# A two-block model in one kernel: handing out the second block's convolution by what is left, and moving eight copies to ScalarE

## The chip, the cores and the metric

The kernel runs on one core of one Trainium2 chip. The metric is device time in microseconds (us) of one execution, and lower is better. Before the change the median of three timed runs is 2483.45 us (2479.06 to 2487.06).

## The reference

The input is x, 512 positions by 1024 channels, float32. Two layers of a first block are followed by one layer of a second block.

A layer of the first block: RMS norm, one projection `h @ w_in`, and three branches, each gated and summed. They are a sliding-window attention with 8 heads, a short convolution of 3 taps, and a state-space model (SSM) with 32 groups of 64 complex states. Then comes a gated feed-forward of 2816 hidden channels.

The second block, cut to what matters here:

```python
h = rms_norm(x, pre_norm1) * (1 + sc1) + sh1
u_glu, q, k, v, gate_logits = split(h @ w_in_2)
u = ua * sigmoid(ub)                       # 1024 channels
u = depthwise_conv(u, 31 taps) + conv_b    # causal, along the 512 positions
u = silu(layer_norm(u, conv_ln_g, conv_ln_b))
y_conv = u @ conv_w_out_2 + conv_b_out
att = (softmax(q1 k1) - lam * softmax(q2 k2)) @ v    # causal, 8 heads
y_att = rms_norm(att, head_norm) * (1 - lam_init)
y = (sigmoid(g_conv) * y_conv + sigmoid(g_att) * y_att) @ w_o
x = x + g1 * rms_norm(y, post_norm1)
```

A feed-forward of 4096 hidden channels ends the block.

## The kernel before, in words

Activations lie with channels on the 128 partitions and positions along the row: eight tiles of 128 x 512, held in a pool of 78 equal slots of SBUF. Freed slots go to the end of a list, and new tiles take from its head. A float32 operand is split into a rounded high part and the rest (`split`, one ScalarE and one VectorE instruction), and a product is three matmuls (`mm3`, L470 to L472): high by high, high by low, low by high.

Weights come as a stream of units of 128 x 1024, three ahead, through rings of three buffers. SyncE loads a unit into `raw`, ScalarE writes the high part `wh`, and VectorE subtracts to get `wl`. For most of the second block's units `wl` is instead made by ScalarE and by a DMA from GpSimd's queue that adds the weights into it.

Beside the big products runs smaller work, written as Python generators that sit in lanes (class `Lane`): "bg" (first block's attention and SSM), "tab" (the SSM's tables, on GpSimd), "conv" and "att" (second block). `fm` and the other product loops call `beat()` after each group of matmuls, and every third beat is a tick. At a tick each lane gains its rate in credit and takes one step of its generators per whole credit. So the rates set where in program order the small work stands between the products. An order for each engine is then worked out by the framework's list scheduler, which takes instructions by program order but may issue a later one that it reckons ready earlier. SyncE keeps program order.

The second block's order: the gated linear units (GLU), whose last ten units run with the convolution lane already under way at rate 0.6 (R3); four parts, each with q, k and v for two heads; 16 gate units, all after part 3; `conv_w_out_2` (eight units), which needs the whole normalized convolution; `w_o_2`.

Counted in ticks by the loops: a part has 48 beats, so 16 ticks; the gates 128 beats, so 43 ticks; `conv_w_out_2` 64 beats, so 21 ticks.

- A channel tile's convolution (`convolve`) is one ScalarE instruction and 30 VectorE multiply-adds over 512 positions, with a step after every three: 10 steps a tile, 80 in all. A sum over the tiles, `csum`, is kept for the mean.
- `conv_norm` follows in the same lane: mean, eight steps of centring and squaring, one of the reciprocal root, and eight steps that scale, apply SiLU and split one tile each: 17 steps. What is left of the lane when the gates are done is issued at once by `finish("conv")`, ahead of `conv_w_out_2`.
- `diff_attention` of a part is one turn of q and k and four blocks of queries. With the steps that a waiting generator spends the four parts have 121 steps. The lane is two wide. Each part's attention is queued at the end of that part.

The rates before: "conv" 0.6 in the four parts (R4), 0.8 in the gates (R5); "att" 1.0 (R2), and 1.5 in `conv_w_out_2` (R6), where tile 6 calls `finish("att")` if attention isn't done.

In the first block `ssm` lays the input of a channel tile `ct` (0 to 3) out anew: 16 copies of 32 x 128, half on ScalarE, half on VectorE (L1176). GpSimd makes the tables of the next tiles meanwhile.

Of the kernel before, what the change touches and what calls it, by code (L numbers as in the profile page):

```python
# [13 lines left out]
AX = mybir.AxisListType  # L14


R1, R2, R3, R4, R5, R6 = 0.9, 1.0, 0.6, 0.6, 0.8, 1.5
T = 512
D = 1024
KD = 8  # L20
# [291 lines left out]
class Net:  # L312
# [839 lines left out]
    def ssm(self, L, ct, u, tabs, ys2):  # L1152
# [8 lines left out]
        bc, bl, cl, er, ei, rt = tabs[ct]  # L1161
# [9 lines left out]
        for i in range(4):  # L1171
            for j in range(4):
                o = uu[32 * j:32 * j + 32, i]
                s = u[32 * i:32 * i + 32, j::4]
                if j % 2:
                    nc.vector.tensor_copy(out=o, in_=s)  # L1176
                else:
                    self.act(o, s)
            if i == 1:
                yield  # L1180
# [191 lines left out]
    def second(self, follow, out):  # L1372
# [3 lines left out]
        conv = []  # L1376
        us = [None] * 8

        def convolve(i):
            acc = self.big(f"acc{i}")  # L1380
            self.act(acc, us[i], AF.Identity, scale=self.cw[:, 31 * i + 30:31 * i + 31], bias=self.p("conv_b", i))
            for j in range(29, -1, -1):
                s = 30 - j
                self.stt(acc[:, s:], us[i][:, :512 - s], self.cw[:, 31 * i + j:31 * i + j + 1], acc[:, s:], ALU.mult, ALU.add)
                if j % 3 == 0:
                    yield
            self.free(us[i])
            conv.append(acc)
            if i == 1:
                csum.append(self.big("csum"))  # L1390
                self.add(csum[0], conv[0], conv[1])
            elif i > 1:
                self.add(csum[0], csum[0], acc)

        csum, cn = [], []
        cl = self.lane("conv", 1, R3)
        ths = {}

# [12 lines left out]
        for i in range(GLU_HELD // 2):  # L1411
            cl.waiting.append(convolve(i))
        for i in range(GLU_HELD // 2, 8):
            w = self.unit("w_in_2")
            pb = self.psum("ub")
            self.fm(pb, w, 0, hs)
            t = self.big("th")
            self.act(t, pb, AF.Tanh, scale=0.5)
            w = self.unit("w_in_2")
            pa = self.psum("ua")  # L1420
            self.fm(pa, w, 0, hs)
            us[i] = self.big(f"uu{i}")
            self.stt(us[i], t, 1.0, pa, ALU.add, ALU.mult)
            self.free(pa, pb, t)
            cl.waiting.append(convolve(i))
            if i == GLU_HELD // 2:
                r1b = self.spread(self.r1)
                for k in range(8):
                    self.spill(k)
# [14 lines left out]
        def gate(m):  # L1444
            w = self.unit("w_in_2")
            pg = self.psum("gate")
            self.fm(pg, w, 0, hs)
            t = self.big("th")
            self.act(t, pg, AF.Tanh, scale=0.5)
            self.free(pg)  # L1450
            if m < 8:
                ga[m] = t
            else:
                gc.append(t)
            combine()
        al = self.lane("att", 2, R2)
        self.lane("conv", 1, R4)
        for part in range(4):
            pq = [self.psum(f"pq{t}") for t in range(NTB)]
            for i in range(4):  # L1460
                wh, wl, _ = self.unit("w_in_2")
                for t in range(NTB):
                    s = slice(128 * t, 128 * t + 128)
                    for e in range(2):
                        k = 2 * i + e
                        self.mm3(pq[t], hs[k][0][:, s], hs[k][1][:, s], wh[e], wl[e], k == 0, k == 7)
                        self.beat()
            ra = [self.big("rope", shape=(128, 8, 64)) for _ in range(NTB)]
            for t in range(NTB):
                self.act(ra[t].rearrange("p h d -> p (h d)"), pq[t])  # L1470
            self.free(pq)
            for t in range(NTB):
                self.rope2(ra[t], cos[:, t], sin[:, t])
            wv = [self.unit("w_in_2") for _ in range(2)]
            vv = []
            for t in range(NTB):
                if t % 2 == 0:
                    ps = self.psum("pv", (128, 2, 256))
                s = slice(128 * t, 128 * t + 128)
                for k in range(8):  # L1480
                    self.mm3(ps[:, t % 2], hs[k][0][:, s], hs[k][1][:, s], wv[k // 4][0][k % 4], wv[k // 4][1][k % 4],
                             k == 0, k == 7)
                    if k % 2:
                        self.beat()
                if t % 2:
                    vv.append(self.big("vv", shape=(128, 2, 256)))
                    self.act(vv[-1].rearrange("p t c -> p (t c)"), ps.rearrange("p t c -> p (t c)"))
                    self.free(ps)
            self.free(wv[0][2], wv[1][2])
            for m in (2 * part, 2 * part + 1):  # L1490
                ya[m] = self.big(f"ya{m}")
            al.waiting += self.diff_attention(part, ra, vv, ya, done)
            if part == 3:
                cl.waiting.append(self.conv_norm(conv, csum, cn))
                self.lane("conv", 1, R5)
            for m in range(sum(GATES[:part]), sum(GATES[:part + 1])):
                gate(m)
        self.free(hs, self.cs2)
        self.finish("conv")
        self.lane("att", 2, R6)  # L1500
        ys = []
        for m in range(8):
            w = self.unit("conv_w_out_2")
# [267 lines left out]
    def conv_norm(self, conv, csum, out):  # L1771
        while len(conv) < 8:
            yield
        s = csum[0]
        ps = self.psum("ssum", (128, 4))
        self.sums(ps, s)
        mu = self.small("mu", (128, 4))
        self.ts(mu, ps, 1.0 / D, ALU.mult)
        self.free(ps)
        mb = self.spread(mu)  # L1780
        st = [None]
        for i in range(8):
            self.sub(conv[i], conv[i], mb)
            self.sq_acc(st, conv[i])
            yield
        self.free(mb)
        rb = self.spread(self.rstd(st))
        yield
        for i in range(8):
            v = conv[i]  # L1790
            self.stt(v, v, self.p("ln_g", i), rb, ALU.mult, ALU.mult)
            t = self.big("th")
            self.act(t, v, AF.Tanh, scale=0.5, bias=self.hb[:, i:i + 1])
            self.act(v, v, AF.Identity, bias=self.p("ln_b", i))
            self.stt(v, t, 1.0, v, ALU.add, ALU.mult)
            h, l = self.big(f"cnh{i}", F32R), self.big(f"cnl{i}", F32R)
            self.split(h, l, v, 0.5)
            self.free(v, t)
            out.append((h, l))
            yield  # L1800
        self.free(rb)
# [49 lines left out]
```

## Time and profile before

| What | us |
|---|---|
| median of three timed runs | 2483.45 |
| lowest and highest | 2479.06, 2487.06 |
| the profiled execution, whole | 2489.97 |
| its span, first to last instruction | 2488.2 |
| TensorE busy (PE in the profile) | 2442.6 |
| VectorE busy (DVE) | 1594.7 |
| ScalarE busy (ACT) | 1111.5 |

The profile is one execution. PE is TensorE, PEld its loading of the stationary operand, DVE is VectorE, ACT is ScalarE, POOL is GpSimd, SP is SyncE. Times of rows count from the span's start. A figure in square brackets is idle time of the engine before a row, with what ended it. PEclk is the share of full clock that TensorE was granted. Where a helper issues an instruction, its line is the helper's: L380 is any ScalarE activation, L383 any two-tensor VectorE or GpSimd operation, L401 any scalar-tensor-tensor operation.

In the second block the GLU's last ten units run from 1643 to 1699 us, the four parts from 1699 to 1859, the gates from 1859 to 1978, and `conv_w_out_2` from 1996 to about 2069.

### The profile page before, as it was taken

To read this page: it belongs to the slowest core of one execution; us is meant where nothing else is said; L and a number is where in the kernel's file an instruction comes from. 1 tells how busy PE (TensorE), PEld (TensorE's weight loads), DVE (VectorE), ACT (ScalarE), POOL (GpSimd) and SP (SyncE) were. 2 spreads that over 40 slices of the span, in tenths; PEclk is the share of its full clock that TensorE was granted. 3 is DMA by queue.
4 is the path that set the end of the run, shared out by engine and by line. 5 is a ranking of instruction groups with operands and counts; after the bars stand their busy time and mean duration, and the time that the engine had idled before them with its cause. 6 is when DMAs were issued, how large, how long until landed. Compare 5 with 4: busy or idle time off the path is not lost.

```text
span 2488.2 us, 32578 instructions
## 1 busy us (share of the span) xinstructions
PE 2442.6 (98%) x12206; PEld 2054.3 (83%) x12206; DVE 1594.7 (64%) x3010; ACT 1111.5 (45%) x2034; POOL 362.5 (15%) x870
## 2 busy tenths in 40 slices
PE   8999999999999999999999999999999999999998
PEld 6888888888888888888888788988887769988887
DVE  7898855544455489875677744688788466643435
ACT  5467433322233365743432222544656765634222
POOL 7824000000037063200000000001111110000000
PEclk9999999999999999999999999999999989999999
DMA  4222233223233322123366632367646543122232
GB/s 154 80 77 69 77 123 106 93 94 102 93 99 109 120 70 79 60 102 121 130 208 223 216 120 94 116 168 182 147 102 140 119 106 119 69 93 89 93 106 77
DMA packets 90879, 282.80 MB, mean 114 GB/s; under 512 B 10336, under 2 KB 11744, under 8 KB 90720
## 3 DMA queue, kind: packets, MB, share of 16 engines
q1 hardware_dynamic: 83520, 254.50, 30.5%
q0 software_dynamic: 7200, 26.22, 6.2%
q8 instruction: 95, 1.56, 0.2%
q14 instruction: 64, 0.52, 0.1%
HBM read 274.39 MB, written 6.29 MB: 113 GB/s over the span
## 4 chain that ended last, share of the span: by engine, by line
PE 80%; DVE 7%; DMA 6%; issue 3%; ACT 2%; POOL 2%; SPq 1%; DVEq 0%; POOLq 0%; ACTq 0%
PE bank L470 25%; PE bank L471 25%; PE bank L472 25%; DMA slot<-in_wada_dram 4%; DVE slot L383 2%; DVE wl L383 2%; ACT slot L380 2%; PE bank L1712 1%; DVE slot L401 1%; DMA raw<-in_w_dram 1%; POOL s_w L383 1%; POOL slot L383 1%; PE bank L1744 1%; DVE slot L1176 0%; PE bank L1202 0%
## 5 line engine op out<-in xcount | busy, mean ns | idle before, releaser
L470 PE MATMUL bank<-slot,wh 128*128 128x512 f32 x2456 | 964.3, 394 | 7.8 <-ACT slot L380 7.6
L472 PE MATMUL bank<-slot,wl 128*128 128x512 f32 x2456 | 959.8, 391 | 4.2 <-DMA wl<-in_w_dram 2.1
L471 PE MATMUL bank<-slot,wh 128*128 128x512 f32 x2456 | 960.2, 391 | 0.0
L380 ACT ACTIVATE wh<-raw 128x1024 fp32r<-128x1024 f32 (+3 forms) x369 | 385.2, 1045 | 767.4 <-PE bank L471 390.6
L470 PEld LDWEIGHTS bank<-slot,wh 128*128 128x128 f32 x2456 | 463.4, 189 | 105.1 <-ACT slot L380 8.3
L472 PEld LDWEIGHTS bank<-slot,wl 128*128 128x128 f32 x2456 | 462.6, 188 | 104.5 <-DVE wl L383 4.9
L471 PEld LDWEIGHTS bank<-slot,wh 128*128 128x128 f32 x2456 | 463.4, 189 | 95.9 <-issue 1.7
L383 DVE TENSOR_TENSOR wl<-raw,wh 128x1024 fp32r<-128x1024 f32 (+3 forms) x319 | 390.9, 1226 | 203.0 <-ACT wh L380 201.6
L383 DVE TENSOR_TENSOR slot<-bank,slot 128x512 f32<-128x512 f32 (+4 forms) x340 | 197.6, 591 | 239.9 <-PE bank L472 208.7
L380 ACT ACTIVATE slot<-slot 128x512 fp32r<-128x512 f32 (+3 forms) x378 | 207.9, 558 | 288.9 <-DVE slot L383 265.9
L383 DVE TENSOR_TENSOR slot<-slot,slot 128x512 f32<-128x512 f32 (+4 forms) x480 | 287.0, 617 | 51.0 <-ACT slot L380 47.5
L380 ACT ACTIVATE slot<-bank 32x128 f32<-32x128 f32 (+8 forms) x398 | 183.2, 473 | 96.9 <-PE bank L472 34.5
L471 PE MATMUL bank<-wl,slot 128*128 128x512 f32 (+1 forms) x480 | 182.4, 380 | 4.3 <-DVE wl L383 4.3
L472 PE MATMUL bank<-wh,slot 128*128 128x512 f32 (+1 forms) x480 | 181.5, 379 | 0.0
L470 PE MATMUL bank<-wh,slot 128*128 128x512 f32 (+1 forms) x480 | 181.4, 380 | 0.0
L470 PE MATMUL bank<-slot,slot 128*128 128x256 f32 (+1 forms) x624 | 177.9, 293 | 2.1 <-ACT slot L380 2.1
L471 PE MATMUL bank<-slot,slot 128*128 128x256 f32 (+1 forms) x624 | 179.0, 291 | 0.5 <-DVE slot L401 0.5
L472 PE MATMUL bank<-slot,slot 128*128 128x256 f32 (+1 forms) x624 | 178.3, 289 | 0.0
L401 DVE SCALAR_TENSOR_TENSOR slot<-slot,slot 128x512 f32<-128x512 f32 (+1 forms) x184 | 123.9, 688 | 84.7 <-DMA slot<-in_wada_dram 57.2
L401 DVE SCALAR_TENSOR_TENSOR slot<-slot,cw,slot 128x485 f32<-128x485 f32 (+24 forms) x240 | 166.6, 732 | 4.2 <-ACT slot L380 2.4
L383 DVE TENSOR_TENSOR slot<-slot,bank 128x512 f32<-128x512 f32 (+1 forms) x104 | 66.1, 643 | 131.0 <-PE bank L472 131.0
L470 PEld LDWEIGHTS bank<-slot,slot 128*128 128x128 f32 x624 | 118.2, 193 | 4.4 <-ACT slot L380 2.7
(199 smaller groups left out, 2263.7 us busy)
## 6 DMA issues: line engine op xcount, KB each, us to landing
raw<-in_w_dram SPq DMA_DIRECT2D x373, 512.0 KB, 3.3
wl<-in_w_dram POOLq DMA_DIRECT2D x50, 512.0 KB, 5.6
slot<-in_wada_dram SPq DMA_DIRECT2D x96, 256.0 KB, 4.9
raw<-in_w_dram SPq DMA_DIRECT2D x32, 448.0 KB, 3.3
slot<-in_x_dram SPq DMA_DIRECT2D x16, 256.0 KB, 3.9
xd<-slot SPq DMA_DIRECT2D x16, 256.0 KB, 6.2
slot<-xd SPq DMA_DIRECT2D x16, 256.0 KB, 3.5
out_dram<-slot SPq DMA_DIRECT2D x8, 256.0 KB, 2.0
```

Of the source, the lines that this page charges most:

```text
L380: return self.nc.scalar.activation(out=out, in_=in_, func=func, scale=scale, **kw)
L383: return (eng or self.nc.vector).tensor_tensor(out=out, in0=a, in1=b, op=op)
L401: return self.nc.vector.scalar_tensor_tensor(out=out, in0=a, scalar=s, in1=b, op0=op0, op1=op1, **kw)
L470: t.matmul(ps, ah, bh, start=start, stop=False)
L471: t.matmul(ps, ah, bl, start=False, stop=False)
L472: t.matmul(ps, al, bh, start=False, stop=stop)
L1712: nc.tensor.matmul(ps[e][:, :w], qk[s][x][rows, tn], qk[2 + s][y][rows, :w], start=i == 0, stop=i == 2)
L1744: nc.tensor.matmul(po[:, e], at[e][:, b], vv[b // 2][:, b % 2, 128 * e:128 * e + 128], start=b == 0, stop=b == n)
```

## The change

Three things change. The convolution lane's rate is worked out ahead of each part as the steps still to do (`steps[0]`, 80 at first) over 16 ticks for each part left and 14 more; over 14 ahead of the gates; and `conv_norm` sets it to 0.7 when it starts. The attention lane keeps one rate, 1.25, to its end. In `ssm` the eight copies of tile `ct` 0 that VectorE made go to ScalarE, in both layers.

```diff
-R1, R2, R3, R4, R5, R6 = 0.9, 1.0, 0.6, 0.6, 0.8, 1.5
+R1, R2, R3 = 0.9, 1.25, 0.6
@@ ssm
-                if j % 2:
+                if j % 2 and ct:
                     nc.vector.tensor_copy(out=o, in_=s)
                 else:
                     self.act(o, s)
@@ convolve
                 if j % 3 == 0:
+                    steps[0] -= 1
                     yield
@@ second
+        steps = [80]
         cl = self.lane("conv", 1, R3)
...
         al = self.lane("att", 2, R2)
-        self.lane("conv", 1, R4)
         for part in range(4):
+            cl.rate = steps[0] / (16 * (4 - part) + 14)
...
             if part == 3:
                 cl.waiting.append(self.conv_norm(conv, csum, cn))
-                self.lane("conv", 1, R5)
+                cl.rate = steps[0] / 14
...
         self.finish("conv")
-        self.lane("att", 2, R6)
@@ conv_norm
         while len(conv) < 8:
             yield
+        self.lanes["conv"].rate = 0.7
```

## Rows read from the trace of the kernel before

**Rows 1.** The page's first part: busy time, share of span, instructions.
```profile
span 2488.2 us, 32578 instructions
PE 2442.6 (98%) x12206; PEld 2054.3 (83%) x12206; DVE 1594.7 (64%) x3010; ACT 1111.5 (45%) x2034; POOL 362.5 (15%) x870
```

**Rows 2.** Windows by stage; busy us and instructions of each engine, clock, DMA.
```profile
core 0: us, PE busy (x) PEld busy (x) DVE busy (x) ACT busy (x) POOL busy (x), PEclk, DMA share, GB/s
42.40:52.70 10.30, 6.04 (x28) 4.76 (x26) 10.17 (x10) 5.75 (x9) 10.30 (x28) 0.91 0.00 1
52.70:57.60 4.90, 4.90 (x12) 3.84 (x13) 3.56 (x2) 0.92 (x2) 4.90 (x9) 0.50 0.73 217
1643.40:1698.70 55.30, 55.30 (x244) 45.42 (x243) 53.18 (x83) 23.85 (x28) 7.73 (x9) 1.00 0.75 174
1698.70:1732.00 33.30, 33.30 (x193) 29.51 (x192) 31.91 (x55) 16.79 (x22) 4.32 (x5) 1.00 0.83 201
1732.00:1859.10 127.10, 127.10 (x760) 106.48 (x759) 96.79 (x224) 72.23 (x158) 15.64 (x17) 1.00 0.52 125
1859.10:1921.00 61.90, 61.90 (x303) 48.32 (x302) 54.76 (x106) 36.76 (x80) 9.04 (x10) 1.00 0.56 121
1921.00:1978.00 57.00, 56.98 (x277) 44.72 (x276) 24.95 (x78) 38.12 (x86) 8.46 (x10) 1.00 0.60 127
1978.00:1995.60 17.60, 8.58 (x59) 6.71 (x57) 12.74 (x32) 15.00 (x32) 3.61 (x4) 0.83 0.33 80
1995.60:1999.80 4.20, 4.16 (x9) 2.98 (x10) 2.71 (x6) 4.20 (x12) 0.00 (x0) 0.50 0.00 0
2023.70:2027.10 3.40, 3.40 (x10) 2.62 (x9) 0.34 (x1) 0.29 (x1) 0.86 (x1) 0.50 1.01 290
2064.60:2068.00 3.40, 3.40 (x18) 3.40 (x17) 3.40 (x6) 3.26 (x8) 0.00 (x0) 0.50 0.20 49
```

**Rows 3.** Timeline of DVE: start, time, form; the norm's last phase.
```profile
1985.89 4.73 DVE L401 SCALAR_TENSOR_TENSOR slot<-slot,slot,slot 128x512 f32<-128x512 f32 x7 [0.38 <-ACT slot L380]
```

**Rows 4.** Timeline of PE, 1952 to 2070 us; in brackets idle before.
```profile
1952.13 0.95 PE L597 MATMUL bank<-ones,slot 128*128 128x1 f32 x8
...
1992.08 0.69 PE L1712 MATMUL bank<-slot,slot 64*128 64x128 f32 x4 [4.50 <-DVE slot L383]
1995.62 0.80 PE L470 MATMUL bank<-slot,wh 128*128 128x512 f32 x1 [1.88 <-ACT slot L380]
...
2022.13 0.50 PE L472 MATMUL bank<-slot,wl 128*128 128x512 f32 x1 [2.12 <-DMA wl<-in_w_dram]
...
2064.07 1.18 PE L1744 MATMUL bank<-slot,slot 128*128 128x128 f32 x6 [2.61 <-ACT slot L380]
```

**Rows 5.** Timelines of DVE, ACT and PE around 45 us, layer 0.
```profile
42.37 8.29 DVE L1176 COPY slot<-slot 32x128 f32<-32x128 f32 x8
50.69 5.57 DVE L383 TENSOR_TENSOR wl<-raw,wh 128x1024 fp32r<-128x1024 f32 x3
...
44.51 1.06 ACT L380 ACTIVATE wh<-raw 128x1024 fp32r<-128x1024 f32 x1 [0.41 <-PE bank L472]
...
47.26 1.18 PE L470 MATMUL bank<-wh,slot 128*128 128x512 f32 x5
52.70 0.79 PE L471 MATMUL bank<-wl,slot 128*128 128x512 f32 x1 [4.26 <-DVE wl L383]
```

**Rows 6.** Tile cw, the convolution: ns min/median/max, first and last start.
```profile
L401 DVE SCALAR_TENSOR_TENSOR slot<-slot,cw,slot x240: 689/732/752, 1634.2 to 1919.2; 128x503 f32<-128x503 f32 x7, 128x497 f32<-128x497 f32 x7, 128x495 f32<-128x495 f32 x7, 128x493 f32<-128x493 f32 x7
```

**Rows 7.** Lines of DVE, 1564 to 2070 us: count, busy us, mean ns.
```profile
L552 DVE CUSTOM_DVE_ANT_0 slot<-bank,slot 128x128 f32<-128x128 f32 (+3 forms) x64 | 30.2, 487 | 32.5 <-PE bank L1712 32.3
L401 DVE SCALAR_TENSOR_TENSOR slot<-slot,dka,slot 128x128 f32<-128x128 f32 (+3 forms) x32 | 16.1, 546 | 0.0
```

**Rows 8.** The same copies elsewhere: eight on DVE, eight on ACT.
```profile
829.13 2.22 DVE L1176 COPY slot<-slot 32x128 f32<-32x128 f32 x8
...
926.22 3.52 ACT L380 ACTIVATE slot<-slot 32x128 f32<-32x128 f32 x8
```

## The prediction

> **What bounds the kernel now.** I read the page first: TensorE is busy 2442.6 of 2488.2 us [rows 1]. Making another engine cheaper gains nothing by itself; only TensorE's idle time, 45.6 us, and the stretches at half clock can be won. So I looked next at where TensorE idles in the stages that the change touches: the windows by stage, then its timeline there.
>
> From 1643 to 1978 us TensorE is idle for 0.02 us in all, though VectorE is busy 53.2 of 55.3 us in the last ten GLU units and 31.9 of 33.3 in part 0 [rows 2]. Then 17.6 us come in which TensorE has 8.6 us of work, so 9.0 idle [rows 2]. In that stretch VectorE and ScalarE work through the last phase of the convolution's norm [rows 3], which `finish("conv")` issues in one go after the gates; the first matmul of `conv_w_out_2` waits for ScalarE until 1995.62 [rows 4]. Two more waits follow: 2.12 us for a weight DMA, 2.61 us for attention's transposes at tile 6 [rows 4]. After each the granted clock is 0.50 for a while: 4.2, 3.4 and 3.4 us [rows 2]. At the lower of the two levels (1.2 against 2.4 GHz) half of each is lost: 2.1 + 1.7 + 1.7 = 5.5 us.
>
> In layer 0 TensorE waits 4.26 us at 52.70 for a weight's low part [rows 5], and 4.9 us at half clock follow [rows 2].
>
> **The change part by part.**
>
> *The convolution's rate.* Followed through the loops, 16 of the 80 steps are done when part 0 begins. Before, 0.6 x 64 ticks bring it to 54 at the gates' start; 26 steps and the 17 of the norm remain, and 43 ticks at 0.8 do 34 or 35, so 8 to 9 are left: the norm's whole last phase. After, the rate is 64 / 78 = 0.82 in all four parts and stays there, since each part works it out anew from what is left; the convolution is done 14 ticks into the gates, and the norm's 17 steps at 0.7 take 24 ticks. It ends at tick 38 of 43, and nothing is left to finish. Nothing is added to any engine. TensorE's gain is the 9.02 us of idle time and the 2.1 us of clock after it: 11.1. Bounds: 0, if the norm is still late, to 11.1.
>
> *What it costs in the parts.* 14.5 convolution steps move from the gates into the parts: 14.5 x 3 x 0.732 us [rows 6] = 31.8 us of VectorE. Attention adds 0.25 x 48 = 12 steps in parts 1 to 3. Its two dearest VectorE groups make (30.2 + 16.1) / 121 = 0.38 us a step [rows 7]; with the smaller operations I estimate 0.6, so 7 us. In the parts VectorE is busy 31.9 + 96.8 of 160.4 us, so 31.7 are idle [rows 2]. TensorE also gets 12 attention steps more there: parts 1 to 3 took 127.1 us against 3 x 33.3 for a part without attention, 27.2 us for 48 steps [rows 2], so 12 x 0.57 = 6.8 us. Demand 38.8, room 38.5: VectorE would be full. What it doesn't manage slips into the gates, where it has 61.9 + 57.0 - 54.8 - 25.0 = 39.1 us free before the norm's new work. That TensorE stays fed beside a VectorE at 96% is shown by the GLU units and part 0 [rows 2], but there nothing on TensorE waits for VectorE within a step; attention's scores do. No row shows a full VectorE beside attention. From below: no wait. From above: each of the 32 score pairs (64 maskings of L552 [rows 7]) waits for one convolution step of 3 x 0.732 = 2.2 us, 70 us. I take 4 us, near the lower end, as the stages closest in load have none; both ends go into the range.
>
> *Attention at 1.25.* Before, 91 ticks at 1.0 do 91 of 121 steps by the gates' end, and 30 are left for `conv_w_out_2`; at 1.5 a tick they aren't through at tile 6. After, 1.25 x 91 = 113 are done, and 8 are left, 7 ticks: under three tiles. The wait at 2064 and its clock go: 2.61 + 1.7 = 4.3 us. What is late next there is `w_o_2`'s first product, which needs tile 7, as it does now without a wait.
>
> *The weight wait at 2022.* ScalarE makes that unit's two halves in the same queue in which it is finishing the norm, and the DMA comes after them. With the norm done earlier ScalarE is free in time, as in the gates, where the same chain never stops TensorE [rows 2]. 2.12 + 1.7 = 3.8 us, between 0 and 3.8. These three places make 11.1 + 4.3 + 3.8 = 19.2 us; less 4, I take 15.
>
> *Eight copies to ScalarE.* In layer 0 VectorE's eight take 8.29 us; undisturbed eight take 2.22 [rows 8], and GpSimd is busy without a gap beside them [rows 2]. The `wl` subtractions stand behind them from 50.69, and TensorE ran out of work at 48.44 [rows 5]. Without the copies the first could start when ScalarE's `wh` is ready, at 45.57. But ScalarE now has the copies: eight take 3.52 us [rows 8]. It was idle 0.41 us ahead of `wh` [rows 5], so if all stand ahead, `wh` ends at 45.57 + 3.52 - 0.41 = 48.7, and `wl` 1.86 later (a third of 5.57 [rows 5]), at 50.5. TensorE, whose five high matmuls of 1.18 us also need that `wh`, then stops about 2.1 us in place of 4.26. If the scheduler puts `wh` between the copies it doesn't stop at all. So 2.2 to 4.3 us of idle time, and up to 2.4 of half clock [rows 2]; I take 5, between 2.2 and 6.7. In layer 1 the copies take 2.2 us on VectorE [rows 8] with no TensorE wait at that place: 0.
>
> The Trainium skill speaks against this part: "SBUF — State Buffer", section "Who interferes with whom", says that GpSimd shares one port pair with VectorE, that whoever comes first keeps it for a whole instruction, and that a VectorE instruction with two SBUF inputs contends too. By that the `wl` subtractions, which have two, would be held in the copies' place; it is the third rival. The trace agrees in part: three of them beside GpSimd took 5.57 us, against 8.29 for the eight copies [rows 5].
>
> The Trainium skill's page "ScalarE: Activation LUTs", section "What ACT_TABLE_LOAD costs", gives 186 ns and 0.833 ns a column for an activation, 93 ns overlapped: 0.2 us a copy, an estimate, 1.6 for eight. By that `wh` would be late by 1.2 us rather than 3.1, and the gain would be about 2 us nearer its upper end. The trace has 0.44 a copy [rows 8], and decides.
>
> **Sum.** 15 + 5 = 20 us off the profiled execution's 2489.97 is 2470. That execution is 6.5 us over the median of the runs, 2483.45; the same 20 us off the median is 2463.5.
>
> **The rivals.**
>
> 1. *The waits move rather than go.* A full VectorE delivers the last convolution tiles late, and the norm's sums, in TensorE's queue ahead of gate matmuls, hold those up; half of the 19.2 us is lost. For it: demand equals room above. Against it: VectorE starts the convolution's last instruction at 1919.2 [rows 6], TensorE the sums at 1952.13 [rows 4], so VectorE is some 30 us ahead; and it idles 32 of the last 57 us of the gates [rows 2]. Gain 9.6 - 4 + 5 = 10.6: 2473.
>
> 2. *Slower.* In parts 1 to 3 and the gates each score pair waits behind convolution steps in VectorE's queue. At 2.2 us a pair it is 70 us; the 24.2 us of gain (without the 4) are used up when a third of it shows, 0.75 us a pair. At half, 35 us: 2483.45 - 24 + 35 = 2494. For it: the balance above. Against it: VectorE was waiting for TensorE's scores 32.3 us in all [rows 7], so it was usually early.
>
> 3. *The copies' change does nothing.* The copies were held 8.29 - 2.22 = 6.1 us [rows 5, 8]. If the first subtraction, ready at 45.57 at the earliest, is held as long in their place, it ends at 45.57 + 6.1 + 1.2 = 52.9, where it ends now. For it: GpSimd has no gap there [rows 2]. Against it: the subtractions behind the copies met the same GpSimd work and took 1.86 us each. The second block alone gives 15 us: 2468.5.
>
> 4. *Nothing is gained*: the norm is still late in `finish`, because the schedule had its place set by VectorE and not by the rates: 5 from the copies, 2478.5.
>
> **How the numbers follow.** Forecast 0.52 (2463.5, its own range 2455 to 2471); rival 1 0.16; rival 2 0.09; rival 3 0.14; rival 4 0.09. 0.3% is 7.5 us, about what a measurement tells from no change. Faster by more: below 2476, that is the forecast, rival 3, nearly all of rival 1, 0.80. Within: rival 4 and what is left, 0.13. Slower: the larger part of rival 2, 0.07. The range: the full 19.2 + 6.7 = 25.9 us give 2457.5, and 4 us are allowed below it for reordering in the first layers, 2453; above, half of rival 1 and rival 4 lie within 2480.
>
> **What would show it.** Right: the gates followed by `conv_w_out_2` without a gap; the norm's last phase among the gates on VectorE's timeline; no wait for a weight DMA or for attention's transposes after it; the convolution's first steps of tile 4 inside part 1. For the copies: sixteen ScalarE copies near 40 us, and at most 2 us of TensorE's wait at 48 to 53. Wrong: idle TensorE in the parts with VectorE as releaser (rival 2), a gap before the sums within the gates (rival 1), or the same 9 us after the gates (rival 4).

## The result and the profile after

The median after is 2497.82 us (2495.30 to 2497.95), against 2483.74 before on the same chip: a ratio of 1.0053 (95% interval 1.0037 to 1.0069), 14 us slower. The forecast was 2463.5 us, with a range from 2453 to 2480. The profiled execution took 2497.84 us, its span is 2496.0.

The page's first part, which answers to [rows 1]:

```profile
span 2496.0 us, 32574 instructions
PE 2448.9 (98%) x12206; PEld 2058.0 (82%) x12206; DVE 1585.3 (64%) x2994; ACT 1119.8 (45%) x2050; POOL 361.0 (14%) x870
```

The windows by stage, which answer to [rows 2]: layer 0 up to the first matmul that had to wait and after it, part 0, parts 1 to 3, the gates in two pieces, and `conv_w_out_2`. It begins here at 2021.1 us, so the second piece of the gates holds its first 8.6 us.

```profile
42.40:49.80 7.40, 4.33 (x20) 3.24 (x18) 1.04 (x2) 7.21 (x17) 7.40 (x27) 0.98 0.00 0
49.80:56.60 6.80, 6.56 (x15) 4.85 (x16) 5.65 (x3) 3.46 (x5) 6.80 (x9) 0.52 0.41 123
...
1698.90:1732.20 33.30, 33.11 (x189) 29.07 (x189) 31.27 (x54) 17.56 (x23) 4.38 (x5) 1.00 0.80 203
1732.20:1877.90 145.70, 141.05 (x801) 115.20 (x800) 119.65 (x277) 79.75 (x185) 15.62 (x18) 0.98 0.43 109
1877.90:1988.00 110.10, 106.10 (x532) 83.22 (x532) 67.03 (x168) 68.35 (x163) 15.89 (x18) 0.97 0.47 106
1988.00:2029.70 41.70, 37.72 (x161) 28.68 (x160) 22.45 (x58) 34.59 (x73) 5.82 (x7) 0.92 0.46 89
2029.70:2078.10 48.40, 45.66 (x224) 37.44 (x224) 31.18 (x56) 32.36 (x60) 5.82 (x7) 1.00 0.83 240
```

TensorE had no idle time in the parts before [rows 2]; now parts 1 to 3 hold 145.70 - 141.05 = 4.7 us of it. Some of the 18.6 us by which they are longer is attention work that used to stand later. VectorE is busy 119.65 of 145.7 us there, 82%: it is not full. The two pieces of the gates still hold 4.0 us of idle time each, 8.0 in all.

What TensorE waited for longest between 1690 and 2180 us (engine and line, releaser: us in total, times, the longest). Lines stand two lower than before: L1714 is the scores, L1738 and L1764 are transposes, L1746 is the product with v.

```profile
PE bank L1746 <- ACT slot L380: 4.0, 2, 2.9
PE bank L472 <- DMA wl<-in_w_dram: 2.7, 2, 1.7
PE bank L1746 <- ACT djk L380: 2.6, 3, 1.1
PE bank L597 <- DVE slot L383: 2.1, 1, 2.1
PE bank L1764 <- ACT slot L380: 1.9, 1, 1.9
PE bank L1714 <- DVE slot L383: 1.5, 3, 0.9
```

All of these but the weights and L597 (in `w_o_2`, as before) are attention's own matmuls, waiting for the answer of ScalarE or VectorE to an earlier matmul of theirs. The norm's gap of [rows 4] is gone. VectorE ends the norm's last phase here beside attention, and TensorE's timeline has waits for attention in that place:

```profile
1997.62 2.50 DVE L401 SCALAR_TENSOR_TENSOR slot<-slot,slot 128x512 f32<-128x512 f32 x4 [0.36 <-ACT slot L380]
```

```profile
2001.44 0.49 PE L1746 MATMUL bank<-slot,slot 128*128 128x128 f32 x2 [2.90 <-ACT slot L380]
...
2003.27 1.22 PE L1746 MATMUL bank<-slot,slot 128*128 128x128 f32 x4 [1.09 <-ACT slot L380]
```

In layer 0, against [rows 5], ScalarE runs the sixteen copies and one more activation in a row, and only then makes `wh`; TensorE waits 3.10 us for it.

```profile
40.95 7.74 ACT L380 ACTIVATE slot<-slot 128x512 f32<-128x512 f32 x17
48.71 2.95 ACT L380 ACTIVATE wh<-raw 128x1024 fp32r<-128x1024 f32 x3
```

```profile
49.82 2.29 PE L470 MATMUL bank<-wh,slot 128*128 128x512 f32 x5 [3.10 <-ACT wh L380]
52.33 0.80 PE L471 MATMUL bank<-wl,slot 128*128 128x512 f32 x1 [0.22 <-DVE wl L383]
```

### The profile page after: what moved, and what is told of

The parts are those of the page before. It is cut to its first block, busy times and chain, and to the rows that moved or that the text cites. A ratio compares the mean times of both kernels' runs of the same rounds, so it can differ in the third digit from the quotient of the medians.

```text
span 2496.0 us, 32574 instructions
## 1 busy us (share of the span) xinstructions
PE 2448.9 (98%) x12206; PEld 2058.0 (82%) x12206; DVE 1585.3 (64%) x2994; ACT 1119.8 (45%) x2050; POOL 361.0 (14%) x870
## 4 chain that ended last, share of the span: by engine, by line
PE 79%; DVE 8%; DMA 6%; ACT 3%; issue 2%; POOL 1%; SPq 1%; DVEq 0%; POOLq 0%; ACTq 0%
PE bank L471 24%; PE bank L472 24%; PE bank L470 24%; DMA slot<-in_wada_dram 4%; DVE slot L383 3%; DVE wl L383 2%; ACT slot L380 2%; DVE slot L401 2%; DMA wl<-in_w_dram 1%; PE bank L1714 1%; PE bank L1746 0%; PE bank L1202 0%; DVE slot L1256 0%; PE bank L1214 0%; DMA raw<-in_w_dram 0%
## 5 line engine op out<-in xcount | busy, mean ns | idle before, releaser
L380 ACT ACTIVATE slot<-slot 128x512 fp32r<-128x512 f32 (+4 forms) x394 | 214.8, 553 | 301.5 <-DVE slot L383 275.3
L380 ACT ACTIVATE slot<-bank 128x512 f32<-128x512 f32 (+6 forms) x398 | 182.5, 474 | 108.0 <-PE bank L472 41.0
L401 DVE SCALAR_TENSOR_TENSOR slot<-slot,cw,slot 128x485 f32<-128x485 f32 (+26 forms) x240 | 166.7, 731 | 5.3 <-PE bank L471 2.0
```

The lines of the kernel that those rows point to most:

```text
L380: return self.nc.scalar.activation(out=out, in_=in_, func=func, scale=scale, **kw)
L401: return self.nc.vector.scalar_tensor_tensor(out=out, in0=a, scalar=s, in1=b, op0=op0, op1=op1, **kw)
```

## The experiments

### The parts of the change by themselves

Four kernels: each part alone, and the two parts of the second block together. The theories, as the expectations name them: A, attention's dependent steps stand too close at 1.25 a tick; B, the convolution's rate fills VectorE; C, the copies.

**copies_only**: the kernel before with

```diff
-                if j % 2:
+                if j % 2 and ct:
```

> Kernel before with the first states' eight copies on ScalarE and nothing else changed. Theory A (the loss comes from attention at 1.25, the copies are nearly neutral): the changed kernel's wait at 49.8 us was 3.10 in place of 4.26 with the same half clock after it, so 1 us less: 2482 to 2484, ratio 0.999 to 1.000. Theory B (full VectorE in the parts, the convolution's rate): the same. Theory C (the copies cost time somewhere later): above 2490.

Measured: 2487.06 us, before 2484.54; ratio 1.0012 (1.0003 to 1.0021). The copies gain nothing and cost 2.5 us, which lies between the range of A and B and that of C.

**att_only**: the kernel before with attention's rates alone.

```diff
-R1, R2, R3, R4, R5, R6 = 0.9, 1.0, 0.6, 0.6, 0.8, 1.5
+R1, R2, R3, R4, R5, R6 = 0.9, 1.25, 0.6, 0.6, 0.8, 1.25
```

> Kernel before with attention at 1.25 a tick throughout, the convolution's rates as before. Theory A (attention's dependent steps stand too close behind each other, and TensorE waits for ScalarE's answers in its queue): TensorE's waits for attention appear in the parts and gates, 4 to 9 us idle and two or three stretches of half clock, and the norm after the gates still costs its 9 us: 2493 to 2502, slower than before. Theory B: the convolution's rate does it, so this one is about the same as before or 2 to 4 us faster, since the wait at tile 6 goes: 2478 to 2484.

Measured: 2504.64 us; ratio 1.0078 (1.0066 to 1.0090). Attention alone costs 20 us, more than the whole change and 2.6 more than A's upper end.

**conv_only**: the kernel after with attention's rates and the copies put back.

```diff
-R1, R2, R3 = 0.9, 1.25, 0.6
+R1, R2, R3, R6 = 0.9, 1.0, 0.6, 1.5
...
-                if j % 2 and ct:
+                if j % 2:
...
         self.finish("conv")
+        self.lane("att", 2, R6)
```

> The convolution's and the norm's rates as in the changed kernel, attention at 1.0 and 1.5 as before, copies as before. Theory A: the norm is out of the way before the gates end and attention is as sparse as before: 11 to 15 us faster than before, 2468 to 2473. Theory B (VectorE full): waits for VectorE in the parts eat it up, 2484 to 2498.

Measured: 2479.97 us; ratio 0.9982 (0.9973 to 0.9990), 4.6 us faster. In the parts, 1692.7 to 1860.4 us, its window shows VectorE busy 147.6 of 167.7 us and TensorE 167.2: a VectorE at 88% costs TensorE 0.5 us. Theory B falls, with attention at 1.0; A's range is missed too, by 7 us. In the gates and in `conv_w_out_2` TensorE still waits, for attention (from 1690 to 2090 us, L1715 the scores, L1747 the product with v):

```profile
PE bank L1747 <- ACT slot L380: 3.5, 2, 2.3
PE bank L1715 <- DVE slot L383: 3.4, 1, 3.4
PE bank L1739 <- DVE slot L401: 1.0, 1, 1.0
```

**no_copies**: the kernel after with the copies put back.

```diff
-                if j % 2 and ct:
+                if j % 2:
```

> The changed kernel with the copies on VectorE as before. Theories A and B: within 2 us of the changed kernel, 2496 to 2500. Theory C: 5 us or more faster than the changed kernel, below 2493.

Measured: 2492.07 us; ratio 1.0034 (1.0022 to 1.0047). Over conv_only that is 12.1 us for attention at 1.25. The time lies in theory C's range and not in that of A and B, so the copies have a share of their own in the change; its size is taken up below. Attention's rate has the larger one.

### Distance or amount

At 1.25 a tick there is more attention in the parts and the gates, and a block's next step also comes sooner. The lane's width tells these apart. A lane takes its generators in turn, so one of them comes round every width / rate ticks: 2.0 before, 1.6 in the change. A wider lane does the same number of steps per tick on more blocks. (A block that still waits for its q and k spends steps without work, and a wider lane has more of those.)

**att_w3**: att_only, three wide.

```diff
-        al = self.lane("att", 2, R2)
+        al = self.lane("att", 3, R2)
...
-        self.lane("att", 2, R6)
+        self.lane("att", 3, R6)
...
-        mx = [self.small("dmx", (128, 2), bufs=4) for _ in range(2)]
+        mx = [self.small("dmx", (128, 2), bufs=6) for _ in range(2)]
```

> Attention alone at 1.25, as in att_only (2504.6 us), but three generators wide instead of two (and six small maxima buffers instead of four), so that the same number of steps per tick is spread over one more block. A generator's next step then comes 3/1.25 = 2.4 ticks after its last one; in before it is 2/1.0 = 2.0, in att_only 2/1.25 = 1.6. Theory A (a block's dependent steps stand too close, TensorE waits in order for ScalarE's and VectorE's answers): most of the 20 us goes, 2481 to 2489, and TensorE's idle time in the gates falls from 22.5 to about 10 us. Rival D (not the distance but the amount: a quarter more attention in these stretches overloads ScalarE and VectorE): it stays near 2504, no better than 2499.

Measured: 2476.45 us, before 2482.49; ratio 0.9975 (0.9966 to 0.9984). The 20 us of loss became 6 us of gain, below the expected 2481 to 2489. The gates up to the last gate product, and the gap from there to the first product of `conv_w_out_2`, first att_only's and then att_w3's:

```profile
1865.70:2010.60 144.90, 131.70 (x648) 103.39 (x648) 94.59 (x229) 85.62 (x205) 20.18 (x23) 0.96 0.48 105
2010.60:2031.30 20.70, 11.40 (x59) 8.29 (x57) 14.79 (x34) 16.22 (x35) 3.31 (x4) 0.75 0.38 123
```

```profile
1870.20:1992.10 121.90, 121.90 (x636) 96.25 (x633) 88.15 (x220) 80.78 (x193) 20.96 (x23) 1.00 0.55 121
1992.10:2008.79 16.69, 5.27 (x25) 2.80 (x24) 13.60 (x33) 16.34 (x35) 1.63 (x2) 0.72 0.37 81
```

VectorE and ScalarE work nearly as much in both kernels' gates. TensorE's idle time there falls from 13.2 us to none, and the granted clock rises from 0.96 to 1.00; the gap holds 9.3 and 11.4 us. TensorE's longest waits between 1690 and 2090 us, att_only's first (lines as in the kernel before, L1712 the scores):

```profile
PE bank L1762 <- ACT slot L380: 7.1, 2, 4.4
PE bank L1712 <- DVE slot L383: 5.7, 2, 4.3
PE bank L1712 <- ACT slot L380: 4.8, 3, 2.3
PE bank L472 <- DMA wl<-in_w_dram: 4.3, 3, 2.2
PE bank L1744 <- ACT djk L380: 2.4, 2, 1.8
```

```profile
PE bank L470 <- ACT slot L380: 9.4, 1, 9.4
PE bank L1712 <- ACT slot L380: 2.0, 1, 2.0
PE bank L472 <- DMA wl<-in_w_dram: 0.4, 1, 0.4
```

What is left in att_w3, 9.4 and 2.0 us, lies in the norm's gap after the gates, which this kernel keeps from before. att_only has that gap too: 6.8 of the 20.0 us that its list gives for attention lie in it. The amount of attention is the same: by the gates' start both kernels have issued 96 of its 192 score matmuls, and by the start of `conv_w_out_2` all. Rival D falls.

**nocop_w3**: no_copies with the first and the last of these three lines (it has no R6 line). 

> The change's second block as it is (convolution by what is left, attention 1.25; copies back on VectorE; 2492.1 us at width 2) with attention three wide. Theory A: attention's 12 us on top of the convolution's rates go, and the norm and weight waits stay away, so 2473 to 2481, the first version that gets most of the predicted gain. Rival D: 2489 to 2495, as at width 2.

Measured: 2472.16 us; ratio 0.9959 (0.9946 to 0.9971), just below A's range. Here too the amount is the same: no_copies and nocop_w3 have issued 96 score matmuls by the gates' start and 180 by the start of `conv_w_out_2`. The gates of no_copies, then nocop_w3's parts and gates:

```profile
1875.10:2017.50 142.40, 134.43 (x649) 104.87 (x649) 85.31 (x212) 97.53 (x224) 20.77 (x24) 0.95 0.47 103
```

```profile
1691.30:1873.60 182.30, 176.01 (x1018) 147.72 (x1017) 160.44 (x351) 100.66 (x220) 21.73 (x24) 0.98 0.51 124
1873.60:1995.20 121.60, 121.60 (x626) 95.20 (x626) 74.23 (x194) 91.85 (x207) 18.62 (x22) 1.00 0.54 117
```

The gates lose all of their idle time. The parts do not: they hold 6.3 us (no_copies 5.4).

**conv_w3**: conv_only with the same edit. 

> The convolution's rates alone (2480.0 us), attention at 1.0 and 1.5 as before but three wide. At width 2 TensorE still idles 6.1 us in the gates and 2.8 in conv_w_out_2, nearly all for attention's answers, with 10.2 us at half clock. Theory A: 3/1.0 = 3 ticks between a block's steps remove most of these, 6 to 12 us: 2468 to 2474. Rival E (these waits come from the norm's work in VectorE's and ScalarE's queues ahead of attention's, whatever the distance): 2478 to 2482.

Measured: 2470.88 us; ratio 0.9955 (0.9943 to 0.9966), some 7 us less than conv_only by the ratios. Rival E falls: with more distance these waits went too (idle time in the gates 0.8 us).

**att_gates**: the kernel before, attention at 1.25 from the gates on.

```diff
                 self.lane("conv", 1, R5)
+                al.rate = 1.25
...
-R1, R2, R3, R4, R5, R6 = 0.9, 1.0, 0.6, 0.6, 0.8, 1.5
+R1, R2, R3, R4, R5, R6 = 0.9, 1.0, 0.6, 0.6, 0.8, 1.25
```

> The kernel before with attention at 1.0 in the parts and 1.25 from the gates on (att_only has 1.25 in the parts too, 2504.6 us). In att_only the idle time is in the gates (22.5 us), hardly in the parts (1.1). Theory A, with the place in the gates: the loss is there whatever the parts do, since 1.25 brings two steps of a block one tick (2.8 us) apart: 2494 to 2506. Rival F (the loss comes from which steps of attention meet the norm and the last convolution steps, so from the shift that the parts' 1.25 makes): 2481 to 2488.

Measured: 2492.70 us; ratio 1.0049 (1.0037 to 1.0061). The gates alone bring half of the loss, a little below A's range and above F's. A's strong form, that the parts don't matter, is wrong, and F is not ruled out as a part of it: which steps meet the norm's work may matter beside the distance.

### Both ends of the distance

**before_w1** and **before_w3**: the kernel before, one and three wide, at its own rates.

```diff
-        al = self.lane("att", 2, R2)
+        al = self.lane("att", 1, R2)
...
-        self.lane("att", 2, R6)
+        self.lane("att", 1, R6)
```

That is before_w1; before_w3 has 3 in both places, and six small maxima buffers.

> The kernel before (rates 1.0 and 1.5) with attention one generator wide: the same number of steps per tick and nothing else, but a block's next step comes 1.0 tick after its last one instead of 2.0. Theory A (distance between a block's dependent steps): far worse than attention at 1.25 and width 2 (1.6 ticks, +20 us): 2510 to 2560, with TensorE waiting for ScalarE and VectorE at attention's own matmuls from the parts on. Rival D (amount per tick): the amount is unchanged, 2478 to 2488.

> The kernel before with attention three wide (3.0 ticks between a block's steps) and its own rates everywhere. TensorE's waits at attention's matmuls in before are 4.5 and 2.6 us, with some 6.8 us at half clock; the gap after the gates (9 us) stays. Theory A: those go, so 5 to 10 us faster, 2473 to 2479. Rival D: 2480 to 2486.

Measured: 2530.57 us, ratio 1.0189 (1.0173 to 1.0204), and 2477.28 us, ratio 0.9975 (0.9963 to 0.9987); before 2483.22. Rival D, that the amount counts, expected no change in either. One wide, TensorE waits in attention, and for weights too (1690 to 2090 us); why the weights come late there was not followed up:

```profile
PE bank L471 <- DMA wl<-in_w_dram: 11.0, 2, 5.6
PE bank L472 <- DMA wl<-in_w_dram: 9.7, 2, 6.9
PE bank L1712 <- DVE dmx L552: 6.0, 3, 4.7
PE bank L1762 <- ACT slot L380: 5.7, 3, 4.0
```

**nocop_w4**: no_copies, four wide (its other small rings of three at four, the maxima at eight). 

> nocop_w3 (2472.2 us) with attention four wide: 4/1.25 = 3.2 ticks instead of 2.4. Its one wait of attention's left is 4.0 us in part 3, with 6.8 us at half clock, some 7 us in all. If distance still counts there: 2464 to 2469. If that wait is of another kind (ScalarE's copies of q, k and v ahead of the answer): 2470 to 2474.

Measured: 2467.78 us; ratio 0.9939 (0.9926 to 0.9953): 15 us faster than before and some 28 faster than the change by the ratios, the fastest of all. Its interval overlaps nocop_w3's. That distance did it isn't shown: the wait at L1764 fell from 4.0 to 1.5 us, but others came in, and from the first part to the last unit of `conv_w_out_2` TensorE is idle for 10.7 of 353.3 us against 6.3 of 357.1 in nocop_w3. The amount changed too: 144 score matmuls by the end of the gates against 180.

**after_w3**: the whole change, three wide. 

> The whole change as it was made, copies on ScalarE too, with attention three wide. By the two parts measured apart: nocop_w3's 2472.2 plus 2.5 to 5.7 us for the copies, 2474 to 2479: faster than before, where the same change two wide was slower. If the copies' loss was tied to how the second block stood: 2470 to 2474.

Measured: 2473.72 us; ratio 0.9960 (0.9946 to 0.9973). The change that was slower is faster than before by one number, the lane's width. Its ratio is that of nocop_w3, so here the copies cost nothing that can be told.

Attention's settings without the copies' edit, in order of the distance, in us against before on the same chip (att_gates, with 2.0 ticks in the parts and 1.6 after them, is at +10):

| width / rate | ticks | convolution as before | convolution by what is left |
|---|---|---|---|
| 1 / 1.0 | 1.0 | +47 (before_w1) | |
| 2 / 1.25 | 1.6 | +20 (att_only) | +8 (no_copies) |
| 2 / 1.0 | 2.0 | 0 (before) | -5 (conv_only) |
| 3 / 1.25 | 2.4 | -6 (att_w3) | -10 (nocop_w3) |
| 3 / 1.0 | 3.0 | -6 (before_w3) | -12 (conv_w3) |
| 4 / 1.25 | 3.2 | | -15 (nocop_w4) |

Neither column rises with the distance, and at three wide 1.0 and 1.25 steps a tick give nearly the same. What a wider lane brings besides, more blocks in flight, more small buffers and other steps beside the norm's, was not separated from the distance.

## Why the prediction was wrong

**The step that failed: "Attention at 1.25."** It counted steps (113 in place of 91 by the gates' end, 8 left) and took the wait at 2064 us [rows 4] as won: 4.3 us. What denser steps cost TensorE in the gates stood at nothing. The wait at tile 6 did go; in att_only's `conv_w_out_2` TensorE waits for weights alone. But measured alone the edit costs 20 us, and 12 on top of the convolution's rates. In att_only's gates TensorE is idle for 13.2 of 144.9 us, where before had 0.02 [rows 2], and the granted clock is 0.96 in place of 1.00: by an estimate from these two, 6 us more.

A step's matmul needs the answer of ScalarE and VectorE to the step before it. Where none of the big products stands between the two in TensorE's order, TensorE stands until the answer has come. The longest such wait in att_only's gates, on TensorE, ScalarE and VectorE in turn:

```profile
1962.37 0.39 PE L472 MATMUL bank<-slot,wl 128*128 128x512 f32 x1
...
1963.67 0.60 PE L1684 MATMUL bank<-cst,slot 128*128 128x128 f32 x4
1966.60 0.49 PE L1712 MATMUL bank<-slot,slot 64*128 64x128 f32 x3 [2.33 <-ACT slot L380]
1971.39 0.69 PE L1712 MATMUL bank<-slot,slot 64*128 64x128 f32 x4 [4.31 <-DVE slot L383]
1972.02 0.79 PE L470 MATMUL bank<-slot,wh 128*128 128x512 f32 x1
```

```profile
1965.93 0.61 ACT L380 ACTIVATE slot<-bank 128x512 fp32r<-128x512 f32 x1
```

```profile
1964.63 4.91 DVE L383 TENSOR_TENSOR slot<-slot,slot 128x512 f32<-128x512 f32 x8 [5.71 <-ACT slot L380]
1969.45 1.29 DVE L401 SCALAR_TENSOR_TENSOR slot<-slot,slot 128x512 f32<-128x512 f32 x2
1970.65 0.68 DVE L383 TENSOR_TENSOR slot<-bank,slot 128x512 fp32r<-128x512 f32 x1
```

At 1963.67 TensorE transposes a piece of q and k. ScalarE writes its high part at 1965.93. The subtraction for the low part stands on VectorE behind eight of the norm's instructions and two more until 1970.65. The scores (L1712) come at 1966.60 and 1971.39, and no product lies between the transposes and them. From 1971.4 to 1976.4 us the granted clock is 0.50. So two things meet in such a wait: other work ahead of the answer, and nothing beside it on TensorE. The rate and the width set the second. The profile of before held a sign of it: its waits of 4.50 and 2.61 us [rows 4] are of this kind. The prediction counted the second as a backlog, and the first, scores that wait for a subtraction behind the norm's instructions of [rows 3], as part of the norm's 9.02 us.

**Rival 2** had the right kind of loss, score pairs that wait in another engine's queue, but tied it to convolution steps and a full VectorE. With attention at 1.0 that is not so: with those steps in the parts conv_only has 0.5 us of idle time there and conv_w3 none. At 1.25 a small part of it came: 5.4 us in no_copies' parts against 1.1 in att_only's, and 6.3 in nocop_w3's against 0.0 in att_w3's, beside a VectorE at 84 to 88%. The longest, 4.05 us in nocop_w3, waits for an answer whose small VectorE instructions come between convolution steps (`cw`), among others:

```profile
1851.56 0.73 DVE L401 SCALAR_TENSOR_TENSOR slot<-slot,cw,slot 128x490 f32<-128x490 f32 x1
1852.20 0.17 DVE L398 TENSOR_SCALAR dss<-dss 128x2 f32<-128x2 f32 x1
...
1853.74 0.73 DVE L401 SCALAR_TENSOR_TENSOR slot<-slot,cw,slot 128x489 f32<-128x489 f32 x1
...
1854.45 0.16 DVE L383 TENSOR_TENSOR dss<-dss,dfin 128x2 f32<-128x2 f32 x1
```

```profile
1855.06 0.48 PE L1764 MATMUL bank<-cst,slot 128*128 128x128 f32 x1 [4.05 <-ACT slot L380]
```

**The convolution's rate**, 11.1 us less some 4 for a full VectorE, with 3.8 for the weight: the mechanism held, the size did not. The gap after the gates is gone, tile 4's first step is at 1742.9 us, inside part 1, and the norm's last phase ran up to 2005 beside attention. But only 4.6 us of it came at width 2, since TensorE now met attention's waits (conv_only: 3.5, 3.4 and 1.0 us). Three wide it is worth 5 us at attention 1.0 (conv_w3 against before_w3, by their ratios 0.9955 and 0.9975) and 4 at 1.25 (nocop_w3 against att_w3): there the gates with the gap are 17.0 us shorter, but the parts, with their 6.3 us of idle time, 9.5 longer. The 4 us for a full VectorE were not there at 1.0; at 1.25 the parts cost more than that. The weight wait at 2022 [rows 4] is gone in conv_only, but the change has 2.7 us of such waits in `conv_w_out_2`.

**The copies**, 5 us to be won: the term was mis-sized because [rows 5] is one execution. Eleven executions with VectorE's copies were profiled, the same instructions in layer 0. In nine the eight copies took 3.70 to 5.31 us and the wait behind them was at most 1.48; in two, that of [rows 5] and before_w1's, they were held longer, with waits of 4.26 and 6.09. An ordinary one (no_copies), VectorE and then TensorE:

```profile
42.70 4.08 DVE L1176 COPY slot<-slot 32x128 f32<-32x128 f32 x8
```

```profile
48.56 0.50 PE L471 MATMUL bank<-wl,slot 128*128 128x512 f32 x1 [0.78 <-DVE wl L383]
```

So usually about 1 us was there to win. The prediction did place the new wait: `wh` at 48.7 was forecast if all copies stand ahead of it, and the first of three was there at 49.8, behind the copies. The waits are 3.3 us in the change, 3.4 in copies_only and 1.8 in after_w3, against about 2.1 forecast for that case. From 48 to 60 us the granted clock is 0.72 in the first two and 1.00 in after_w3, as in no_copies. The cost lies between nothing (after_w3 against nocop_w3) and some 5 us (the ratios 1.0053 and 1.0034, whose intervals overlap), and no comparison shows a gain.

The Trainium skill, "SBUF — State Buffer", section "Who interferes with whom", has VectorE, in modes that a copy can enter, and GpSimd share a port pair that whoever comes first keeps for a whole instruction. The trace agrees in part: one copy of the eight holds most of the spread, 4.32 us in before and 4.31 in before_w1 against 1.33 to 2.38 in the nine others, but sixteen GpSimd instructions run beside it in before, not one. Why it was held longer in two executions stays open. Rival 3, a subtraction held as long in the copies' place, did not come: the three took 5.65 us in the change and 5.57 before [rows 5].

**Put together**, the forecast had 10.9 us for the convolution's rates with the weight, 4.3 for attention and 5 for the copies: 20 faster. The runs have 4.6 won (conv_only), 12.1 lost (no_copies) and some 5 lost (the change), which is near the 14 us measured.

## What to carry to other kernels

A rate at which dependent small work is laid between big products sets two things: how much of it gets done, and how far a step stands from the one whose answer it needs. Work out both; if the distance (width over rate) falls towards the time that the answer takes, with the other work in the queues ahead of it, take more independent blocks in turn instead of more steps of the same ones. A short stall read from one profiled execution is worth its size only if a second execution shows it.

## What was not expected of the hardware

The same eight VectorE copies of 32x128 beside GpSimd took 3.70 to 8.29 us from one execution to another, and most of the difference sits in a single copy (1.33 to 4.32 us). ScalarE's sixteen of them took 6.8 us, 0.427 each; by the Trainium skill's "ScalarE: Activation LUTs", section "What ACT_TABLE_LOAD costs", 0.2 us each was estimated, and the measurement decides.
